# A hybrid attention block: when the steps of three attention branches are written among projections, gates and merges

## The chip, the cores and the metric

The kernel runs on one core of a Trainium2 chip. The core has five engines that work side by side: TensorE (PE in the rows; its weight loads are PEld), VectorE (DVE), ScalarE (ACT), GpSimd (POOL) and SyncE (SP, which here only issues transfers). Each engine takes its instructions in the order in which they stand and waits at each for what it needs. The metric is the device time of one execution in microseconds (us), as the median of several runs.

## What is computed

One layer of a hybrid block on 512 positions of width 1024: a norm, one wide projection, three kinds of attention (A sparse, B with compressed and windowed keys, C dilated), three gates that mix their outputs, an output projection and a gated feed-forward part.

```python
h = _rms(x, norm1_g[layer])
(a_q, a_k, a_v, i_q, i_k, i_w, b_q, b_kv, b_g, c_qkv, mix_g) = _split_last(h @ w_in[layer], IN_SIZES)
...
y_a = _dsa_attention(a_q, a_k, a_v, ..., rel_a) @ w_branch_a[layer]
...
y_b = _nsa_attention(b_q, ..., b_gates, ..., rel_b) @ w_branch_b[layer]
...
y_c = _dilated_attention(_rms(c_qkv[:, :, 0], qk[4]), _rms(c_qkv[:, :, 1], qk[5]), c_qkv[:, :, 2],
                         rel_c) @ w_branch_c[layer]
g = jax.nn.sigmoid(mix_g).reshape(bsz, seq, 3, D_MODEL)
x = x + (g[:, :, 0] * y_a + g[:, :, 1] * y_b + g[:, :, 2] * y_c) @ w_out[layer]
h = _rms(x, norm2_g[layer])
gate, up = jnp.split(h @ w_ffn_in[layer], 2, axis=-1)
x = x + (jax.nn.silu(gate) * up) @ w_ffn_out[layer]
```

The dilated branch has three groups of four heads; a position attends to its near 128 positions, to every 4th of the last 512 and to every 16th of the last 2048, and the three are mixed by their softmax sums.

## The kernel before

**Matmuls.** Each product of two float32 matrices is made of three matmuls (helper `mm3`, lines 106 to 108): both operands are split into a high part (`whi`, `xh`) and a low part (`wlo`, `xl`), and high by high, low by high and high by low are summed in one PSUM tile `pm`. Weights come from DRAM as `raw` (issued by SP, line 93), ACT casts the high part (line 81), and DVE subtracts to get the low part (line 82).

**The projection.** `proj_tm` makes 256 columns of the wide projection for four blocks of 128 positions: for each block a `pm` tile, a copy out of it by ACT, and one call of `tick()`. `spill` uses it for what is written to DRAM and read back later: queries of branch A (`aq_tm`), six pieces of queries and keys of branch C (`cqk_tm`) and three of its values (`cv_tm`).

**Attention as a task.** `attention()` is a generator. `start` puts it in a list of tasks, and each `tick()` moves every task of the list by one step, so what a step emits stands in the program between the matmuls that the caller is emitting. It is started behind the first of the two `aq_tm` projections. Its `pipeline` of units is worked three deep: a step emits part `a` of a new unit, part `b` of the one before it, and `c` of the one before that if there is one. Part `a` makes logits on PE (tile `lg`, lines 363 and 364 for A and B, 838 and 843 for C) and a softmax: DVE adds the bias table and takes the extreme (line 547 by name of the helper `add_table`), ACT takes the exponential, DVE the reciprocal and the normalisation (lines 563, 564 for A and B; 855, 856 for C); in A the bias table is first masked by POOL (`tabm`, line 557). Part `b` transposes the probabilities `p` or `pc_` on PE (tile `tr`, line 111) and copies them out (`pT` by ACT, in C also `pt12` by DVE, line 876). Part `c` makes the products with the values (`ovb`, `ova`, `ovc`). Units of B come first, then A, then C: `c_prep` reads back `c_in` from DRAM (line 755), transposes it on PE, and makes the queries and keys `cqs`, `cks` (split in two by ACT and DVE, lines 765 to 781) and `cq`; it also loads bias tables `ctab` by many small transfers (line 246) and clears three tiles `pt12` on POOL (line 825). Branch C has two halves `hf` of eight units; `c_prep` of the second half is fed in between the units of the first. There are 86 steps in all.

**Gates and merges.** Then come, for the branches in the order B, A, C (`bi` = 1, 0, 2) and eight column blocks `f` each, a `gate` (24 matmuls, `xh` and `xl` against `whi` and `wlo`, with two ticks, then a tanh by ACT into a `tz` tile that shares three buffers of tag `tm`) and a `merge` (12 matmuls of the branch's output `oT`, or 6 for C, then a multiply by DVE; from A on the sum so far is read from `dz` in DRAM and added). The result is stored to `dz` by SP (line 978), but for C, where it stays on chip. Ahead of a branch's first merge `ready(bi)` ticks until the attention outputs of that branch are all there, and ahead of the third until no task is left.

**What sets the order.** The order on each engine comes from the tile framework's scheduler, which runs the program with a model of the engines: of the instructions that are ready it takes by priority, and priority follows the order of emission. Parts `c` stand in `tc.high_priority()`. The logits have two PSUM buffers and the transposes two; `p`, `pc_` and `c_in` share five buffers in SBUF. Output projection and feed-forward come behind all that and have no attention in them.

Of the kernel before, what the change touches and what calls it, by code (L numbers as in the profile page):

```python
# [31 lines left out]
C_CQ, C_CK, C_CV, C_MIX = 2268, 3036, 3804, 4572  # L32
# [35 lines left out]
def block_kernel(ctx: ExitStack, tc: tile.TileContext, x, norm1_g, norm2_g, w_in, qk_norm_g, cmp_pos, cmp_w,  # L68
                 w_ba, w_bb, w_bc, w_out, w_fi, w_fo, rel_bias, onehot, masks, out):
    nc = tc.nc  # L70
# [13 lines left out]
    def weights(w, segs, kcs, per=2, pool=()):  # L84

        res = {}
        width = sum(n for _, n in segs)
        with tc.high_priority():
            for k0 in kcs[::per]:
                raw = wp.tile([128, per, width], F32, name="raw", tag="raw", bufs=5)  # L90
                o = 0
                for c0, n in segs:
                    nc.sync.dma_start(raw[:, :, o:o + n],
                                      w[k0 * 128:(k0 + per) * 128, c0:c0 + n].rearrange("(k p) c -> p k c", p=128))
                    o += n
                hi = wp.tile([128, per, width], F32R, name="whi", tag="whi")
                lo = wp.tile([128, per, width], F32R, name="wlo", tag="wlo")
                split(hi, lo, raw, nc.gpsimd if pool and k0 // per % 4 in pool else None)
                for j in range(per):
                    res[k0 + j] = (hi[:, j, :], lo[:, j, :])  # L100
        return res

    def mm3(ps, pairs, k0=0, n=None):
        n = n or len(pairs)
        for j, ((ah, al), (bh, bl)) in enumerate(pairs, k0):
            nc.tensor.matmul(ps, ah, bh, start=(j == 0), stop=False)  # L106
            nc.tensor.matmul(ps, ah, bl, start=False, stop=False)  # L107
            nc.tensor.matmul(ps, al, bh, start=False, stop=(j == n - 1))  # L108
# [7 lines left out]
    def start(gen):  # L116
        tasks.append(gen)

    def tick():
        for g in list(tasks):  # L120
            try:
                next(g)
            except StopIteration:
                tasks.remove(g)
# [79 lines left out]
    def mm_tile():  # L204
        return mmp.tile([128, S], F32, name="pm", tag="mm")
# [43 lines left out]
        return bass.AP(tensor=tab.tensor, offset=tab.offset + hi - 1, ap=[list(tab.ap[0]), [-1, hi - lo]])  # L249


    def proj_tm(segs, evac, then=None):
        width = sum(n for _, n in segs)
        wk = weights(w_in, segs, list(range(KC)), pool=PP)
        for t in range(NT):
            ps = mm_tile()
            ts = slice(t * 128, (t + 1) * 128)
            mm3(ps[:, 0:width], [((xh[:, k, ts], xl[:, k, ts]), wk[k]) for k in range(KC)])
            evac(t, ps)
            tick()  # L260
        if then is not None:
            start(then())

# [20 lines left out]
    def tmt(name):  # L284
        return ap_.tile([128, NT, 256], F32, name=name, tag="tm", bufs=3)

    def norm_heads(tm, c0, nh):

        ss = ty.tile([128, 16], F32, name="ss", tag="ss")
        v4 = tm[:, :, c0:c0 + 64 * nh].rearrange("p t (h d) -> p t h d", d=64)  # L290
        for t in range(0, NT, 2):
            sq = ap_.tile([128, 2, 256], F32, name="sq", tag="sq", bufs=1)
            nc.scalar.activation(sq[:, :, 0:64 * nh], tm[:, t:t + 2, c0:c0 + 64 * nh], AF.Square)
            nc.vector.tensor_reduce(out=ss[:, t * nh:(t + 2) * nh].rearrange("p (t h) -> p t h", h=nh),
                                    in_=sq[:, :, 0:64 * nh].rearrange("p t (h d) -> p t h d", d=64), op=ALU.add,
                                    axis=AX.X)
        r = rstd(ss, NT * nh, 1.0 / 64)
        r4 = r[:, 0:NT * nh].rearrange("p (t h) -> p t h", h=nh).unsqueeze(3).to_broadcast([128, NT, nh, 64])
        nc.vector.tensor_tensor(out=v4, in0=v4, in1=r4, op=ALU.mult)
# [190 lines left out]
    def b_keys(si):  # L490
        ktm = tmt("bk_tm")
        vv = ab.tile([128, NT, 128], F32, name=f"bv{si}")
        bv[si] = vv

        def evac(t, ps):
            nc.scalar.copy(undup(ktm[:, t, :], 2), dup(ps[:, 0:128], 2))
            nc.vector.tensor_copy(vv[:, t, :], ps[:, 128:256])

        def then():
            norm_heads(ktm, 0, 4)  # L500
            yield from wait(3)
            bk[si] = []
            for g in range(2):
                bk[si].append(k_stack(ktm, 128 * g, gain[:, 3:4]))
                yield

        proj_tm([(C_BKV + 256 * (si + 1), 256)], evac, then=then)
# [224 lines left out]
    dC = dp.tile([6, 128, NT, 256], F32, name="dC")  # L732
    dV = dp.tile([3, S, 256], F32, name="dV")
    cmap = {}

    def spill(name, segs, dst, nh):
        t_ = tmt(name)

        def then():
            if nh:  # L740
                norm_heads(t_, 0, nh)
            nc.sync.dma_start(dst, t_)
            yield

        proj_tm(segs, lambda t, ps: nc.scalar.copy(t_[:, t, :], ps[:, 0:256]), then=then)

    c_in = {}
    c_jobs = [(hf, g, s) for hf in range(2) for g in range(3) for s in "qk"]
# [210 lines left out]
    def merge(bi, f, tz):  # L959
        nk = KC // 2 if bi < 2 else 2  # L960
        os_ = outs[bi]
        cs = slice(128 * (f % 2), 128 * (f % 2) + 128)
        th, zi = tz[:, 0, :], tz[:, 1, :]
        if f % 2 == 0:
            wys["w"] = weights(wbs[bi], [(f // 2 * 256, 256)], list(range(nk)))
        if bi != 1:
            nc.sync.dma_start(zi, dz[f])
        wy = wys["w"]
        py = mm_tile()
        mm3(py, [((wy[k][0][:, cs], wy[k][1][:, cs]), (os_[k][:, 0, :], os_[k][:, 1, :])) for k in range(nk)])  # L970
        if bi == 0 or f % 2:
            tick()
        nc.vector.scalar_tensor_tensor(out=th, in0=th, scalar=1.0, in1=py, op0=ALU.add, op1=ALU.mult)
        if bi != 1:
            eng = nc.vector if bi == 2 and f > KC - 3 else nc.gpsimd
            eng.tensor_tensor(out=th, in0=th, in1=zi, op=ALU.add)
        if bi != 2:
            nc.sync.dma_start(dz[f], th)
        else:
            nc.scalar.mul(zs["h"][:, f, :], th, 0.5)  # L980
            nc.vector.scalar_tensor_tensor(out=zs["l"][:, f, :], in0=th, scalar=0.5, in1=zs["h"][:, f, :].bitcast(F32),
                                           op0=ALU.mult, op1=ALU.subtract)
# [15 lines left out]
    cn = 0  # L998
    for hf in range(2):
        for g in range(3):  # L1000
            spill("cqk_tm", [(C_CQ + 256 * g + 128 * hf, 128), (C_CK + 256 * g + 128 * hf, 128)], dC[cn], 4)
            cmap["q", hf, g], cmap["k", hf, g] = (cn, 0), (cn, 128)
            cn += 1
    for g in range(3):
        spill("cv_tm", [(C_CV + 256 * g, 256)], dV[g].rearrange("(t p) c -> p t c", p=128), 0)
    zx = ExitStack()

    def ready(bi):
# [99 lines left out]
    for c in range(0, DFF, 256):  # L1108
# [7 lines left out]
        for j in range(2):  # L1116
# [7 lines left out]
            f = c // 128 + j  # L1124
# [40 lines left out]
```

## Time and profile before

| | us |
|---|---|
| median of three runs | 996.48 |
| the three runs | 994.18, 996.48, 1000.4 |
| the profiled execution | 995.54 |
| its span on the core | 993.8 |
| PE busy | 974.3 |
| DVE busy | 568.1 |
| ACT busy | 437.5 |
| POOL busy | 175.4 |

The times in the rows are those of the profiled execution, counted from the start of its span. The program's parts lie in it roughly so: norm and first projections to 150, the projections of the dilated branch with attention B from there to 283 and their tail to 308, gates and merges of B with attention A to 446, and gates and merges of A with attention C to 545; the third branch's gates and merges and the rest follow. "Busy" of PE counts an instruction's whole duration, and those of two neighbours overlap; the granted clock is 1.00 at the full 2.4 GHz and 0.50 at 1.2 GHz.

### The profile page before, as it was taken

What the parts mean: (1) busy time and instruction counts of PE and PEld (TensorE: products, weight loads), DVE (VectorE), ACT (ScalarE), POOL (GpSimd) and SP (SyncE); (2) the same over time, 40 slices, a digit from 0 to 9 for tenths busy, and PEclk for the clock granted to TensorE, in tenths of its full rate; (3) what the DMA queues carried; (4) which work ended last, traced back from release to release, by engine and by line L of the source; (5) the groups of instructions that cost most, each with busy time, mean ns of one, the idle gap of its engine ahead of it and who ended that gap; (6) DMA issues with size and microseconds to landing.
All of it is one profiled execution on the core that took longest, in us unless ns stands there. A gap on an engine that the chain in (4) does not pass through costs nothing.

```text
span 993.8 us, 16076 instructions
## 1 busy us (share of the span) xinstructions
PE 974.3 (98%) x5887; PEld 827.0 (83%) x5887; DVE 568.1 (57%) x1277; ACT 437.5 (44%) x956; POOL 175.4 (18%) x156
## 2 busy tenths in 40 slices
PE   6999999999999999989999999999999999999998
PEld 6889999899887578858777899988888888888886
DVE  6699999766665655665764654544344444422321
ACT  5544555755665555554543434433233233322220
POOL 4135555543100202231110312000000000000000
PEclk9999999999999899989999999999999999999999
DMA  8541344433232334346613462233333323332421
GB/s 210 122 128 44 85 119 132 123 109 122 90 104 67 85 117 138 107 141 193 180 62 97 140 210 86 85 94 108 96 85 105 107 85 91 110 97 96 138 75 42
DMA packets 119264, 109.91 MB, mean 111 GB/s; under 512 B 19931, under 2 KB 105234, under 8 KB 119186
## 3 DMA queue, kind: packets, MB, share of 16 engines
q1 hardware_dynamic: 116994, 107.85, 37.4%
q10 hardware_dynamic: 2192, 1.05, 0.4%
q8 instruction: 46, 0.75, 0.3%
q14 instruction: 32, 0.26, 0.1%
HBM read 96.66 MB, written 12.21 MB: 110 GB/s over the span
## 4 chain that ended last, share of the span: by engine, by line
PE 96%; DMA 1%; DVE 1%; ACT 1%; issue 0%; SPq 0%; DVEq 0%; ACTq 0%
PE pf L108 14%; PE pf L107 14%; PE pf L106 14%; PE pm L107 13%; PE pm L106 13%; PE pm L108 13%; PE tr L111 5%; PE ovb L541 2%; PE lg L363 2%; PE lg L364 2%; PE ova L541 1%; PE lg L843 1%; DMA raw<-in_w_in 1%; PE ovc L888 1%; PE lg L838 0%
## 5 line engine op out<-in xcount | busy, mean ns | idle before, releaser
L82 DVE TENSOR_TENSOR wlo<-raw,whi 128x512 fp32r<-128x512 f32 (+1 forms) x243 | 182.5, 756 | 147.7 <-ACT whi L81 146.6
L81 ACT CAST whi<-raw 128x512 fp32r<-128x512 f32 (+1 forms) x288 | 176.8, 619 | 173.9 <-PE pf L108 78.6
L107 PE MATMUL pm<-wlo,xh 128*128 128x256 f32 (+1 forms) x512 | 145.9, 288 | 0.3 <-DVE wlo L82 0.3
L108 PE MATMUL pm<-whi,xl 128*128 128x256 f32 (+1 forms) x512 | 145.3, 286 | 0.5 <-POOL xl L82 0.5
L106 PE MATMUL pm<-whi,xh 128*128 128x256 f32 (+1 forms) x512 | 145.7, 289 | 0.0
L107 PE MATMUL pf<-xl,whi 128*128 128x512 f32 (+1 forms) x384 | 142.6, 372 | 0.1
L106 PE MATMUL pf<-xh,whi 128*128 128x512 f32 (+1 forms) x384 | 142.5, 372 | 0.0
L108 PE MATMUL pf<-xh,wlo 128*128 128x512 f32 (+1 forms) x384 | 142.0, 371 | 0.0
L107 PEld LDWEIGHTS pm<-wlo,xh 128*128 128x128 f32 x512 | 98.5, 193 | 1.9 <-issue 0.8
L108 PEld LDWEIGHTS pm<-whi,xl 128*128 128x128 f32 x512 | 98.7, 193 | 1.4 <-POOL xl L82 0.8
L106 PEld LDWEIGHTS pm<-whi,xh 128*128 128x128 f32 x512 | 98.3, 194 | 0.4
L107 PE MATMUL pm<-xl,whi 128*128 128x512 f32 x224 | 88.8, 396 | 0.0
L108 PE MATMUL pm<-xh,wlo 128*128 128x512 f32 x224 | 88.6, 395 | 0.0
L106 PE MATMUL pm<-xh,whi 128*128 128x512 f32 x224 | 88.4, 395 | 0.0
L107 PEld LDWEIGHTS pf<-xl,whi 128*128 128x128 f32 x384 | 72.3, 188 | 12.8 <-DVE xl L82 0.3
L108 PEld LDWEIGHTS pf<-xh,wlo 128*128 128x128 f32 x384 | 72.2, 188 | 12.6
L106 PEld LDWEIGHTS pf<-xh,whi 128*128 128x128 f32 x384 | 72.2, 188 | 12.3
L82 POOL TENSOR_TENSOR wlo<-raw,whi 128x512 fp32r<-128x512 f32 x45 | 62.2, 1402 | 111.6 <-ACT whi L81 100.8
L106 PE MATMUL pf<-whi,hh 128*128 128x512 f32 x176 | 69.4, 395 | 0.0
L108 PE MATMUL pf<-whi,hl 128*128 128x512 f32 x176 | 69.4, 395 | 0.0
L107 PE MATMUL pf<-wlo,hh 128*128 128x512 f32 x176 | 69.4, 395 | 0.0
L562 ACT ACTIVATE p<-p,m 128x128 f32<-128x128 f32 (+3 forms) x96 | 53.9, 562 | 28.6 <-DVE m L547 26.4
(312 smaller groups left out, 1702.3 us busy)
## 6 DMA issues: line engine op xcount, KB each, us to landing
raw<-in_w_in SPq DMA_DIRECT2D x92, 256.0 KB, 3.0
raw<-in_w_ffn_in SPq DMA_DIRECT2D x88, 256.0 KB, 2.9
raw<-in_w_ffn_out SPq DMA_DIRECT2D x44, 256.0 KB, 2.8
raw<-in_w_in SPq DMA_DIRECT2D x52, 128.0 KB, 2.4
x<-in_x SPq DMA_DIRECT2D x8, 512.0 KB, 5.9
tab<-dvec SPq DMA_DIRECT2D x16, 256.0 KB, 3.3
dz<-tz SPq DMA_DIRECT2D x16, 256.0 KB, 2.4
tz<-dz SPq DMA_DIRECT2D x16, 256.0 KB, 3.3
```

The costliest lines, as they stand in the source:

```text
L81: nc.scalar.copy(dst_hi, src)
L82: (eng or nc.vector).tensor_tensor(out=dst_lo, in0=src, in1=dst_hi.bitcast(F32), op=ALU.subtract)
L106: nc.tensor.matmul(ps, ah, bh, start=(j == 0), stop=False)
L107: nc.tensor.matmul(ps, ah, bl, start=False, stop=False)
L108: nc.tensor.matmul(ps, al, bh, start=False, stop=(j == n - 1))
L111: nc.tensor.transpose(dst, src, ident[0:src.shape[0], 0:src.shape[0]])
L363: nc.tensor.matmul(lg, qs, k[:, 0, 0:w], start=True, stop=False)
L364: nc.tensor.matmul(lg, qs, k[:, 1, 0:w], start=False, stop=stop)
L541: mm = nc.tensor.matmul(ov[64 * j:64 * j + 64, 128 * b:S], v(b), pts[j][:, 4 * b:3 * b + NT, :], start=first and b == 0, stop=last and b = ...
L562: nc.scalar.activation(p[:, 0:w], p[:, 0:w], AF.Exp, bias=m[:, 0:1], scale=-1.0, accum_out=m[:, 1:2])
L843: nc.tensor.matmul(lg[32 * r:32 * r + 32, c:c + n], ld["q", g][hp, 128 * i + 32 * r:128 * i + 32 * r + 32], ld["k", g][hp, 128 * r:128 * r ...
L888: nc.tensor.matmul(ov[h, 128 * b_:128 * q1], ld["v", 0][:, b_, h], d["pt", jj][:, 2 * b_:b_ + q1, :], start=b_ == 0, stop=False)
```

## The change

`proj_tm` gets an argument `more`: in the first `more` of its four blocks two ticks are called instead of one. `spill` hands it on, and the nine spills of the dilated branch pass 1, so each of these projections emits five steps of the tasks where it emitted four. In `merge` the tick is called always; before, the merges of `bi` = 1 and `bi` = 2 called it only for odd `f`. In the merges of `bi` = 2 there is no task left to step. Nothing else is different; no instruction is added or removed.

```diff
--- before.py
+++ after.py
@@ -249,7 +249,7 @@
         return bass.AP(tensor=tab.tensor, offset=tab.offset + hi - 1, ap=[list(tab.ap[0]), [-1, hi - lo]])
 
 
-    def proj_tm(segs, evac, then=None):
+    def proj_tm(segs, evac, then=None, more=0):
         width = sum(n for _, n in segs)
         wk = weights(w_in, segs, list(range(KC)), pool=PP)
         for t in range(NT):
@@ -257,7 +257,8 @@
             ts = slice(t * 128, (t + 1) * 128)
             mm3(ps[:, 0:width], [((xh[:, k, ts], xl[:, k, ts]), wk[k]) for k in range(KC)])
             evac(t, ps)
-            tick()
+            for _ in range(1 + (t < more)):
+                tick()
         if then is not None:
             start(then())
 
@@ -733,7 +734,7 @@
     dV = dp.tile([3, S, 256], F32, name="dV")
     cmap = {}
 
-    def spill(name, segs, dst, nh):
+    def spill(name, segs, dst, nh, more=0):
         t_ = tmt(name)
 
         def then():
@@ -742,7 +743,7 @@
             nc.sync.dma_start(dst, t_)
             yield
 
-        proj_tm(segs, lambda t, ps: nc.scalar.copy(t_[:, t, :], ps[:, 0:256]), then=then)
+        proj_tm(segs, lambda t, ps: nc.scalar.copy(t_[:, t, :], ps[:, 0:256]), then=then, more=more)
 
     c_in = {}
     c_jobs = [(hf, g, s) for hf in range(2) for g in range(3) for s in "qk"]
@@ -968,8 +969,7 @@
         wy = wys["w"]
         py = mm_tile()
         mm3(py, [((wy[k][0][:, cs], wy[k][1][:, cs]), (os_[k][:, 0, :], os_[k][:, 1, :])) for k in range(nk)])
-        if bi == 0 or f % 2:
-            tick()
+        tick()
         nc.vector.scalar_tensor_tensor(out=th, in0=th, scalar=1.0, in1=py, op0=ALU.add, op1=ALU.mult)
         if bi != 1:
             eng = nc.vector if bi == 2 and f > KC - 3 else nc.gpsimd
@@ -998,11 +998,11 @@
     cn = 0
     for hf in range(2):
         for g in range(3):
-            spill("cqk_tm", [(C_CQ + 256 * g + 128 * hf, 128), (C_CK + 256 * g + 128 * hf, 128)], dC[cn], 4)
+            spill("cqk_tm", [(C_CQ + 256 * g + 128 * hf, 128), (C_CK + 256 * g + 128 * hf, 128)], dC[cn], 4, 1)
             cmap["q", hf, g], cmap["k", hf, g] = (cn, 0), (cn, 128)
             cn += 1
     for g in range(3):
-        spill("cv_tm", [(C_CV + 256 * g, 256)], dV[g].rearrange("(t p) c -> p t c", p=128), 0)
+        spill("cv_tm", [(C_CV + 256 * g, 256)], dV[g].rearrange("(t p) c -> p t c", p=128), 0, 1)
     zx = ExitStack()
 
     def ready(bi):
```

By the code, 49 steps of attention have been emitted at the end of the projections where 40 had, 53 ahead of the first merge where 44 had, and 77 ahead of the first merge of the second branch where 64 had. Attention has no step left from the merge f = 3 of the second branch on; before, that was f = 7.

The next rows show where that moved instructions and where not. Numbers behind names count tiles in the order of the program and so differ between the two; lines behind the first part of the file are one higher after the change. The first place is PE where the last units of branch A stand ahead of the gates: logits of A, transposes of its probabilities, one transpose of a `c_in`, the product. Before:

```order
L363 MATMUL lg_5260<-kst_823,qst_5000 128x512
L364 MATMUL lg_5260<-kst_823,qst_5000 128x512
L111 MATMUL tr_5239<-ident_82,p_5207 128x128 x3
L111 MATMUL tr_5244<-ident_82,p_5218 128x128 x3
L111 MATMUL tr_5287<-ident_82,p_5254 128x128 x4
L111 MATMUL tr_5293<-ident_82,p_5265 128x128 x4
L111 MATMUL tr_5408<-ident_82,c_in_5283 128x128 x4
L541 MATMUL ova_5377<-pT_5137,av_248 64x512
```

After:

```order
L364 MATMUL lg_5020<-kst_823,qst_4787 128x512
L365 MATMUL lg_5020<-kst_823,qst_4787 128x512
L111 MATMUL tr_4999<-ident_82,p_4967 128x128 x3
L111 MATMUL tr_5004<-ident_82,p_4978 128x128 x3
L111 MATMUL tr_5047<-ident_82,p_5014 128x128 x4
L111 MATMUL tr_5053<-ident_82,p_5025 128x128 x4
L111 MATMUL tr_5153<-ident_82,c_in_5043 128x128 x4
L542 MATMUL ova_5125<-pT_4897,av_248 64x512
```

The rows are the same but for numbers, and so are all of PE's 687 instructions around them, from the first logits behind the third product of branch B on to row 2564 below.

The second place is PE behind it, at the head of the units of branch C. `pm_6026` before and `pm_6314` after are the same gate, `cq`, `cqs` and `cks` the prepared queries and keys. Before:

```order
L111 MATMUL tr_5555<-ident_82,c_in_5474 128x128 x4
L107 MATMUL pm_5953<-oT_5386,whi_5776 128x512
L108 MATMUL pm_5953<-oT_5386,wlo_5777 128x512
L106 MATMUL pm_6026<-xh_105,whi_5833 128x512
L107 MATMUL pm_6026<-xl_106,whi_5833 128x512
L108 MATMUL pm_6026<-xh_105,wlo_5834 128x512
L111 MATMUL tr_5574<-ident_82,c_in_5511 128x128 x4
L843 MATMUL lg_5642<-cq_5509,cq_5472 32x32 x4
L843 MATMUL lg_5700<-cq_5509,cq_5472 32x32 x4
L106 MATMUL pm_6026<-xh_105,whi_5833 128x512
L107 MATMUL pm_6026<-xl_106,whi_5833 128x512
L108 MATMUL pm_6026<-xh_105,wlo_5834 128x512
```

After, where the rows on from 2568 to 2603 (36 of them) are all of this kind, transposes, logits and one product, and the gate's first matmul is row 2604:

```order
L111 MATMUL tr_5274<-ident_82,c_in_5222 128x128 x4
L107 MATMUL pm_6298<-oT_5134,whi_6190 128x512
L108 MATMUL pm_6298<-oT_5134,wlo_6191 128x512
L111 MATMUL tr_5320<-ident_82,c_in_5243 128x128 x4
L844 MATMUL lg_5384<-cq_5241,cq_5220 32x32 x4
L844 MATMUL lg_5441<-cq_5241,cq_5220 32x32 x4
L111 MATMUL tr_5373<-ident_82,c_in_5371 128x128 x4
L844 MATMUL lg_5384<-cq_5325,cq_5279 32x32 x4
L844 MATMUL lg_5441<-cq_5325,cq_5279 32x32 x4
L839 MATMUL lg_5492<-cks_5186,cqs_5158 128x256 x2
L844 MATMUL lg_5492<-cq_5241,cq_5220 32x64 x4
L844 MATMUL lg_5492<-cq_5325,cq_5279 32x64 x4
```

Before, the gate's matmuls stand among the transposes and logits; after, they stand behind 36 rows of attention. From the gate on, attention and gates alternate as before, in fewer and longer pieces (18 changes from attention to a gate or merge where there were 27), up to about 545 us by the rows of before.

The third place is SP, which issues the transfers. `dz<-tz` are stores of merged sums, `c_in` and `ctab` loads for branch C's second half, `raw` weights, `c_v` its values. Before:

```order
L755 DMA c_in_5629<-dC_254 128x4x128
L978 DMA dz_256<-tz_5476 128x512
L93 DMA raw_6203<-in_w_in 128x2x256
L813 DMA c_v_5730<-dV_255 128x4x128
L978 DMA dz_256<-tz_5581 128x512
L813 DMA c_v_5868<-dV_255 128x4x128
L967 DMA tz_5766<-dz_256 128x512
L93 DMA raw_6405<-in_w_branch_a 128x2x256
L813 DMA c_v_5966<-dV_255 128x4x128
```

After:

```order
L756 DMA c_in_5585<-dC_254 128x4x128
L246 DMA ctab_5721<-dvec_247 32x128
L246 DMA ctab_5721<-dvec_247 32x256
L246 DMA ctab_5721<-dvec_247 32x128 x2
L756 DMA c_in_5658<-dC_254 128x4x128
L246 DMA ctab_5721<-dvec_247 32x256
L246 DMA ctab_5721<-dvec_247 32x128 x2
L978 DMA dz_256<-tz_5761 128x512
L978 DMA dz_256<-tz_5906 128x512
L978 DMA dz_256<-tz_6061 128x512
L968 DMA tz_6180<-dz_256 128x512
```

The stores to `dz` stood between the loads and now stand three in a row behind the last `ctab` and `c_in` loads of the second half.

## Rows read from the trace of the kernel before

**Rows 1.** The page's first part: busy us, share of the span, instructions, by engine

```profile
PE 974.3 (98%) x5887; PEld 827.0 (83%) x5887; DVE 568.1 (57%) x1277; ACT 437.5 (44%) x956; POOL 175.4 (18%) x156
```

**Rows 2.** Table by stage: window, length, busy us by engine, PEclk, DMA share, GB/s

```profile
150.00:308.00 158.00, 158.00 (x1195) 143.98 (x1193) 109.18 (x308) 95.16 (x256) 49.94 (x36) 1.00 0.37 108
...
324.00:340.00 16.00, 13.82 (x73) 7.93 (x70) 7.81 (x27) 8.42 (x23) 0.67 (x1) 0.79 0.18 55
...
430.00:446.00 16.00, 11.45 (x54) 6.89 (x53) 10.39 (x19) 7.44 (x17) 4.50 (x6) 0.79 0.53 150
...
459.00:545.00 86.00, 85.94 (x681) 64.70 (x680) 52.90 (x153) 39.86 (x89) 7.84 (x6) 1.00 0.46 139
```

**Rows 3.** The same table in slices of 2 us, in both holes

```profile
328.00:330.00 2.00, 1.04 (x7) 0.73 (x7) 1.07 (x6) 2.00 (x8) 0.00 (x0) 1.00 0.63 181
...
336.00:338.00 2.00, 2.00 (x12) 1.12 (x10) 0.00 (x0) 0.00 (x0) 0.00 (x0) 0.50 0.00 0
...
436.00:438.00 2.00, 1.27 (x6) 0.80 (x6) 1.60 (x7) 1.89 (x5) 0.00 (x0) 0.50 0.06 18
```

**Rows 4.** Timeline, all engines, 430 to 437: start, length, engine, line, operation, [idle before]

```profile
431.37 4.02 DVE L564 TENSOR_SCALAR p<-p,m 128x384 f32<-128x384 f32 x1
...
432.44 2.74 POOL L825 MEMSET pt<- 128x1024 f32 x3
...
435.54 0.87 PE L111 MATMUL tr<-ident,p 128*128 128x128 f32 x3 [3.49 <-DVE p L564]
...
436.59 0.41 DVE L564 TENSOR_SCALAR p<-p,m 128x384 f32<-128x384 f32 x1
```

**Rows 5.** Operations on tile `cv_tm`: ns min/median/max, first and last start

```profile
L745 ACT COPY cv_tm<-pm x12: 347/365/376, 227.3 to 282.6; 128x256 f32<-128x256 f32 x12
```

**Rows 6.** Chain of waits, 301 to 312: start, length, what

```profile
308.34 2.31 PE ovb L541 x16
```

**Rows 7.** Timeline, 168 to 170

```profile
168.28 0.33 DVE L633 TENSOR_TENSOR pc<-pc,mc 128x128 f32<-128x128 f32 x1
...
169.22 0.27 PE L111 MATMUL tr<-ident,pc 128*128 128x128 f32 x1
```

**Rows 8.** Chain of waits, 455 to 545, units of branch C

```profile
472.25 0.43 PE lg L838 x2
472.68 0.36 PE lg L843 x16
473.04 0.43 PE pm L108
473.47 0.23 PE pm L106
...
484.57 0.44 PE tr L111 x4
```

**Rows 9.** Groups by line and shape, 440 to 545: busy us, mean ns, idle before

```profile
L781 DVE SCALAR_TENSOR_TENSOR cks<-tr,gain_qk,cks 64x512 fp32r<-64x512 f32 x8 | 6.0, 748 | 0.1
...
L956 ACT ACTIVATE tz<-pm 128x512 f32<-128x512 f32 x8 | 4.8, 596 | 13.2 <-PE pm L108 6.8 <-DMA dz<-tz 5.6 <-POOL tz L976 0.7
...
L766 DVE TENSOR_TENSOR cqs<-tr,cqs 64x512 fp32r<-64x512 f32 x4 | 2.8, 689 | 0.1
...
L855 DVE RECIPROCAL mcc<-mcc 128x1 f32<-128x1 f32 x16 | 2.6, 160 | 1.9 <-ACT pc__6057 L854 0.9 <-ACT pc__6318 L854 0.6 <-ACT pc__6175 L854 0.2
...
L876 DVE COPY pt<-tr 64x128 f32<-64x128 f32 x8 | 2.3, 286 | 0.1
```

**Rows 10.** Timeline of DVE, 491 to 493

```profile
492.09 0.48 DVE L547 CUSTOM_DVE_ANT_1 pc__6016<-lg,ctab,mcc 128x256 f32<-128x256 f32 x1
492.50 0.08 DVE L547 DVE_READ_ACCUMULATOR2_ANT mcc<- 128x1 f32 x1
```

**Rows 11.** Timeline of SP, 456 to 459

```profile
457.54 0.53 SPq L755 DMA_DIRECT2D c_in<-dC  x1
```

**Rows 12.** DMA issues: count, KB each, median us to landing

```profile
c_in<-dC SPq DMA_DIRECT2D x12, 256.0 KB, 3.4
```

## The prediction, made before the kernel was run

> **What bounds the kernel now.** I read the page's list of engines first. PE is busy 98% of the span and nothing else is over 57% [rows 1], so the change can only give or cost what PE idles, what it works at the lower clock, and what its pieces lose where they alternate. The table by stage says where that is [rows 2]: PE is busy all of 150 to 308 us. It has lost time at 324 to 340 (13.82 of 16 busy, granted clock 0.79) and at 430 to 446 (11.45 of 16, clock 0.79); then it is full again from 459 to 545 (85.94 of 86), the stretch in which attention's third branch lies between gates and merges.
>
> The two holes come from the short tails of branches B and A, where PE has only attention left and each step waits for the one ahead of it. Slices of 2 us show PE falling to 1.04 busy and the clock at 0.50 behind it, up to 338 [rows 3]. In the second hole the timeline gives the cause: a DVE normalisation that takes 0.41 us next to it took 4.02 us, while POOL ran a masked table and three clears of `pt12` one behind the other, up to 435.2; PE stood 3.49 us for it [rows 4]. The price of a hole is the idle time and half of the work done at half clock. A mean clock of 0.79 over 16 us is 0.21 x 16 / 0.5 = 6.7 us at 0.50, in each. The first: 16 - 13.82 = 2.2 us idle, and PE full in the slow part (2.00 of 2 at 336 [rows 3]), some 6.4 us of work, so 3.2; together 5.4. The second: 16 - 11.45 = 4.55 idle, and the slow part only some 60% full (1.27 of 2 at 436 [rows 3]), 4 us of work, so 2.0; together 6.6. All a better placing of attention can win here is about 12 us.
>
> **Is emission the limit?** The last copy of the last projection of the dilated branch lies at 282.6 us [rows 5], and by the code 40 attention steps have been emitted by then, the third product of branch B (step 36) among them; that product runs at 308.34 us [rows 6], some 25 us later. Attention runs behind its emission already, held by its own chain (logits, DVE, exp, DVE, transpose, copy) and its buffers, not by when it was written. More steps emitted ahead then change priorities in the scheduler and not the pace, and the order shows just that.
>
> **The change, part by part.** (1) Nine more steps in the nine projections, one each, and four more in the merges of the first branch (f = 0, 2, 4, 6); the eight merges of the third have no task left. No instruction is added or removed on any engine; no price of its own.
>
> (2) 150 to 308 us. The order moves by a few rows only: each logits group up to some 40 matmuls earlier, each transpose about as far behind. PE had no idle here [rows 2]. The tightest hand-over I find is DVE's compressed probabilities, done at 168.28 + 0.33, read by PE at 169.22: 0.6 us of slack [rows 7]. In the new order DVE has up to 1.1 us more ahead of the same transpose, so PE may wait 0 to 0.5 us there. I take 0.3.
>
> (3) 308 to 459 us. On PE the rows from the first logits behind the third product to the merge ahead of the dilated queries' transposes are the same 687 instructions in the same order, on DVE, ACT, POOL and SP likewise (the order pieces show the end of the second hole), and their waits lead to the same producers. The clears of `pt12` stand where they stood. Both holes stay: gain 0. What would have been the win of this change (12 us) is not in it.
>
> (4) 459 us on. Here the order does change (the second pair of pieces). Before, the units of the dilated branch lay between gate matmuls; now 36 rows of attention stand in one run, from the transpose of `c_in_5243` to the next gate, with no gate or merge matmul among them. PE's own work in the run is 38 transposes at 0.11 (0.44 for four) and the logits of eight units, whole or in part (0.43 for the wide pair, 0.18 and more for eight narrow ones), with one product: 4.2 and some 6 us, with the changes between them 10.5 [rows 8]. What it waits for is DVE, in order. With two logits buffers PE may not write the third group before DVE has read the first. From the first read up to that of the seventh unit, DVE has 12 reads of logits (0.48 for the widest, 5.3 by their widths), 12 accumulators (0.08: 1.0), 6 reciprocals (1.0), 6 normalisations (about 0.41 [rows 4]: 2.4), 6 copies to `pt12` (1.7), 2 splits of `cqs` (1.4) and 4 of `cks` (3.0), durations from [rows 9, 10]: 15.8 us. DVE starts each some 0.05 before the one ahead has ended (0.48 from 492.09, the next at 492.50 [rows 10]), so 14. It waits three times for ACT (an exp, twice `cks`), by the tanh's 0.60 [rows 9] 1.9 in all. Behind that stand one more exp and the gate's tanh, 0.6 to 0.7 each, which frees the PSUM tile that the next gate needs, and some 0.5 of hand-overs: 17.3 to 18 us from the first read to the gate. PE has its 10.5 in that time and idles 7. Ahead of it the transpose of `c_in_5371` waits: SP issued the load in its place at 457.54 before [rows 11], behind 24 `ctab` loads; one store ahead of it is gone, so 457.0; it lands 3.4 us later, at 460.4 [rows 12], and PE is there at 459.5: 0.9. Together 7.9 us. Below: DVE's 14 alone, 3.3. Above: no overlap on DVE, 9.7.
>
> (5) The stores `dz<-tz` have moved on SP behind all of the second half's `ctab` and `c_in` loads (third pair). The tanh named above needs a `tm` buffer, free when a store has landed: at 0.53 an issue [rows 11] SP gets there at about 475, and a store has landed by 478.4 if it needs what a load needs [rows 12]; the tanh is due at 477.8. About even; I take nothing, up to 1 more.
>
> (6) The clock. In both holes PE stood, in short pieces in the first and for 3.49 us in the second [rows 4], and its clock was at 0.50 for some 6.7 us afterwards. In the run the 7.9 us fall, queue by queue, into some nine waits of 0.3 to 1.7 us within 19 us, PE 58% busy. In the first hole PE was about half busy ahead of the fall [rows 3]. If it falls here for 6.7 us, 58% of that is 3.9 us of work at half speed, 3.9 us at most where all is on the path, 0 where DVE hides it. I take the middle, 2. The Trainium skill (TensorE: Matmul & The Clock Gate, What's actually happening) has the array throttled only after an idle window and released by activity; read to the letter, waits broken by work would keep the clock up and the sum would be 2 less. The first hole speaks against that reading: the 2 us ahead of its fall hold seven instructions and 1.04 us of work [rows 3]. So the rows decide.
>
> (7) PE goes from attention to gate and merge matmuls 27 times in this stretch before and 18 times after. A first matmul behind logits holds the chain for 0.43, others for 0.23; behind transposes none is longer [rows 8]. So each of the 9 gives between 0 and 0.20; I take 0.08, a gain of 0.7. Behind that the rest of attention is spread between gates again, as now, and the gates and merges that follow stand alone; PE is full in the stretch that has both [rows 2], so nothing more is lost or won.
>
> Sum on the profiled execution's 995.54 us (span 993.8): + 0.3 + 7.9 + 2 - 0.7 = 1005.0. That execution is 0.9 us under the median of the runs, 996.48; a measurement of this kernel tells about 1% from no change, 986.5 to 1006.4.
>
> **Rivals.** *The holes close.* If attention really came earlier, both holes would fill: 995.5 - 12 = 984, faster. For it: that is where the only idle time is. Against: the order there is the same row by row. What could still do it is the clears' timing: the Trainium skill (SBUF — State Buffer, Who interferes with whom) gives DVE and GpSimd one port pair that either locks for a whole instruction, and the 4.02 us row agrees. Should the normalisation start ahead of POOL's row, 3.6 us of wait and some 2 of slow clock go: 995.5 + 9.5 - 5.6 = 999.4. The point that decides is which of the two starts first at 431.3; nothing ahead of it moves. Chance for a result under 986.5: 0.06.
>
> *The run costs little.* DVE's 14 us alone and no fall of the clock, or the holes' own luck as above: 995.5 + 3.3 - 0.7 = 998 to 1001. For it: hand-overs overlap more than I count. Chance 0.27.
>
> *The run costs more.* All bounds up, and the clock falls twice, or the stores of (5) come 2 us late and gates wait for `tm` buffers: 995.5 + 0.5 + 9.7 + 1 + 3.9 = 1010.6. For it: the second hole cost more than its chain of durations. Against: POOL is idle in the run, so no DVE row is stretched. Chance 0.15.
>
> **The numbers.** Forecast 0.52, 1005, own range 1002 to 1008, of which a little under half (0.22) lies above 1006.4. Faster 0.06; slower 0.22 + 0.15 = 0.37; within 1% 0.30 + 0.27 = 0.57. The range 998 to 1011 leaves out 0.06 below, and some 0.1 at the two ends.
>
> **What would show it.** In the profile after: the wait of 3.5 us for the normalisation and both stretches of clock 0.50 as before (3); PE under 60% busy for some 19 us from about 459, its waits on DVE and ACT at transposes and logits of the dilated branch, DVE nearly full in it (4); a third stretch at 0.50 near 465 to 475 (6); PE full elsewhere. It would be wrong if the holes are gone, if DVE is idle while PE waits in the run (then SP's loads were late), or if PE idles between 150 and 308.

## The result and the profile after

Five executions of the changed kernel took 1005.26 to 1007.41 us, median 1007.12; five of the kernel before had a median of 994.68. The ratio is 1.0109, with a 95% interval of 1.0090 to 1.0129: slower by about 1%. The forecast was 1005.0 with 998 to 1011, and the place and the sign were right. Several parts of the sum were not, as the stages show.

The profiled execution took 1006.88 us. The page's first lines, which answer to [rows 1]: the span is 11.3 us longer with the same number of matmuls.

```profile
span 1005.1 us, 16082 instructions
...
PE 977.7 (97%) x5887; PEld 830.3 (83%) x5887; DVE 561.3 (56%) x1277; ACT 438.4 (44%) x956; POOL 175.5 (17%) x156
```

The table by stage, which answers to [rows 2] (columns as there):

```profile
150.00:308.00 158.00, 156.86 (x1187) 142.69 (x1186) 104.43 (x301) 93.32 (x250) 51.21 (x36) 1.00 0.36 107
...
324.00:340.00 16.00, 13.57 (x85) 8.30 (x84) 10.35 (x37) 10.87 (x33) 2.05 (x3) 1.00 0.24 67
...
430.00:446.00 16.00, 11.49 (x51) 6.78 (x50) 9.51 (x16) 7.66 (x17) 4.30 (x5) 0.79 0.57 161
446.00:459.00 13.00, 12.75 (x81) 10.41 (x79) 6.03 (x9) 4.71 (x8) 3.07 (x3) 1.00 0.33 80
459.00:545.00 86.00, 80.27 (x611) 60.59 (x612) 49.20 (x149) 37.84 (x84) 7.74 (x6) 0.86 0.42 123
```

PE has lost 1.14 us in 150 to 308, where it lost none. The first hole is as empty as before (13.57 of 16 busy) but its granted clock stayed at 1.00. The second hole is the one of before (11.49, 0.79). In 459 to 545 PE, full before, is 80.27 of 86 busy at a mean clock of 0.86.

Fixed points of the order say how much each stage took. The third product of branch B in the chain of waits, which answers to [rows 6], starts at 309.61 where it started at 308.34, 1.3 us late:

```profile
309.61 2.31 PE ovb L542 x16
```

The last product of branch A on PE's timeline, the changed kernel's row and then that of before, is 1.6 us early, so the first hole gave back 2.9:

```profile
438.99 3.22 PE L542 MATMUL ova<-pT,av 128*64 128x512 f32 x16
```

```profile
440.59 2.37 PE L541 MATMUL ova<-pT,av 128*64 128x512 f32 x16
```

Its 3.22 us against 2.37 are the low clock of the second hole, which costs 0.85 more here. So the kernel comes out of it 0.8 us early and ends 11.3 us late: **12.1 us are lost among the units of branch C**.

PE's timeline of the long stretch, 457 to 484 (start, length, operation, in brackets the idle time before it and what ended it), shows its waits: 0.65 + 1.58 + 2.10 + 0.56 + 0.78 + 0.31 = 6.0 us.

```profile
457.93 0.60 PE L111 MATMUL tr<-ident,c_in 128*128 128x128 f32 x4
...
459.40 0.63 PE L111 MATMUL tr<-ident,c_in 128*128 128x128 f32 x4 [0.65 <-DMA c_in<-dC]
...
461.83 0.77 PE L839 MATMUL lg<-cks,cqs 128*128 128x256 f32 x2 [1.58 <-DVE mcc L548]
...
466.59 1.11 PE L111 MATMUL tr<-ident,c_in 128*128 128x128 f32 x4 [2.10 <-DMA c_in<-dC]
...
471.43 1.09 PE L111 MATMUL tr<-ident,c_in 128*128 128x128 f32 x4 [0.56 <-issue]
473.30 0.69 PE L111 MATMUL tr<-ident,pc__5452 128*128 128x128 f32 x2 [0.78 <-DMA ctab<-dvec]
...
475.23 0.88 PE L111 MATMUL tr<-ident,pc__5503 128*128 128x128 f32 x3 [0.31 <-DVE pt L877]
...
483.56 0.79 PE L106 MATMUL pm<-xh,whi 128*128 128x512 f32 x1
```

Three of them, 3.5 us, the profile puts down to a transfer (`c_in`, `c_in`, `ctab`). DVE's timeline says the same of the longest from the other side: it had finished at 465.7 and stood for 2.48 us, until 468.17.

```profile
465.26 0.42 DVE L857 TENSOR_SCALAR pc__5503<-pc__5503,mcc 128x384 f32<-128x384 f32 x1
468.17 0.42 DVE L548 CUSTOM_DVE_ANT_0 pc__5549<-lg,ctab 128x256 f32<-128x256 f32 x1 [2.48 <-PE tr L111]
```

The load behind it in the chain of waits: SP went from issue to issue without a pause and came to this `c_in` at 461.36, and the data took 5.19 us. That is 1.0 over the median of 4.2 for this kernel's twelve such loads, with the DMA engines all but full (shares of 0.82 to 1.04 from 460 to 466, two of these slices below), so part of the lateness is the transfer's own.

```profile
460.35 0.42 SPq L246
...
461.36 5.19 DMA c_in<-dC
```

Slices of 2 us show the clock: at 0.50 from some 461.2 to 485, and for the last 9 us of it with PE full.

```profile
458.00:460.00 2.00, 1.35 (x32) 0.93 (x33) 0.69 (x1) 1.44 (x3) 0.00 (x0) 1.00 1.06 303
460.00:462.00 2.00, 0.42 (x18) 0.34 (x18) 1.56 (x8) 1.16 (x3) 0.00 (x0) 0.80 0.82 217
...
464.00:466.00 2.00, 0.49 (x16) 0.24 (x12) 1.06 (x5) 0.71 (x2) 0.00 (x0) 0.50 0.95 266
...
476.00:478.00 2.00, 2.00 (x22) 1.36 (x22) 1.82 (x9) 1.42 (x5) 0.00 (x0) 0.50 0.59 161
...
482.00:484.00 2.00, 2.00 (x16) 1.82 (x16) 1.76 (x7) 1.28 (x3) 0.00 (x0) 0.50 0.92 283
484.00:486.00 2.00, 2.00 (x8) 1.53 (x8) 1.48 (x5) 1.25 (x4) 1.28 (x1) 0.73 0.22 83
```

By the mean of the 86 us, (1 - 0.86) x 86 / 0.5 = 24 us at half clock. PE's own work from the transposes at 457.93 to the gate at 483.56, forecast at 10.5 us, took 25.6 - 6.0 = 19.6. So the slow clock cost about 9 us, say 8 to 10, and the waits 6.0; that is 2 to 4 more than the 12.1 lost, which the fewer changes between attention and gates, and the gates that now stand alone, gave back. That part has not been measured by itself.

### The profile page after: what moved, and what is told of

Same layout as the page of the kernel before. It is cut to its first block, busy times and chain, and to the rows that moved or that the text cites. A ratio compares the mean times of both kernels' runs of the same rounds, so it can differ in the third digit from the quotient of the medians.

```text
span 1005.1 us, 16082 instructions
## 1 busy us (share of the span) xinstructions
PE 977.7 (97%) x5887; PEld 830.3 (83%) x5887; DVE 561.3 (56%) x1277; ACT 438.4 (44%) x956; POOL 175.5 (17%) x156
## 4 chain that ended last, share of the span: by engine, by line
PE 91%; DVE 3%; DMA 3%; issue 1%; SPq 1%; ACT 1%; POOL 1%; DVEq 0%; POOLq 0%; ACTq 0%
PE pf L108 14%; PE pf L107 13%; PE pf L106 13%; PE pm L107 12%; PE pm L106 12%; PE pm L108 12%; PE tr L111 5%; PE ovb L542 2%; PE lg L364 2%; PE lg L365 2%; PE ova L542 1%; DMA raw<-in_w_in 1%; PE lg L844 1%; PE ovc L889 1%; DMA c_in<-dC 1%
## 5 line engine op out<-in xcount | busy, mean ns | idle before, releaser
L82 DVE TENSOR_TENSOR wlo<-raw,whi 128x512 fp32r<-128x512 f32 (+1 forms) x243 | 176.1, 730 | 151.4 <-ACT whi L81 150.1
```

The source lines that it names most:

```text
L82: (eng or nc.vector).tensor_tensor(out=dst_lo, in0=src, in1=dst_hi.bitcast(F32), op=ALU.subtract)
```

## The experiments

The theory going in: one long stretch of attention without gates makes PE wait for DVE, and the waits bring the clock down. The rivals: SP's late loads; the number of steps as such; the clock as something apart. All kernels compare with the kernel before on the same chip; its median there was 996.03 for the first four, 994.42 for the next four, and 994.19 for the last two.

**Each part alone.** The kernel before with only the second part of the change:

```diff
-        if bi == 0 or f % 2:
-            tick()
+        tick()
```

> The kernel before with one part of the change alone: a tick in every merge, no extra tick in the projections. PE's order is that of before up to the units of branch C, and among these no stretch of attention longer than 46 matmuls and transposes stands between two gates (121 in the changed kernel). Theory of the prediction (the loss sits in that one long stretch): nothing is lost, 993 to 997 us as before, and PE waits under 1 us from 459 to 545. Rival (each extra step costs its share of the 11 us, 4 of 13 steps): about 998.5 us, with new waits of some 3 us at transposes of branch C.

Measured: 994.71 us, ratio 0.9989 (0.9969 to 1.0009): no change. The theory's forecast held. The other part alone was not run: built without the ticks in the merges, the changed kernel has every engine's instructions in the same order, row for row. So the projections' steps are the whole change. With fewer of them, counted from the first projection, the order is the changed kernel's from five extra steps on; with three or four it is one and the same again, and the first stretch in branch C has 44 matmuls and transposes instead of 121. Four, in the first four projections:

```diff
-            spill("cqk_tm", [...], dC[cn], 4, 1)
+            spill("cqk_tm", [...], dC[cn], 4, int(cn < 4))
...
-        spill("cv_tm", [...], ..., 0, 1)
+        spill("cv_tm", [...], ..., 0, 0)
```

> The changed kernel with the extra step in only the first four of the nine projections (merges all tick). PE's order up to the units of branch C is then that of the changed kernel, but the first stretch of attention there has 44 matmuls and transposes between gates, not 121; with five or more extra steps the order is the changed kernel's to the row. Theory (the loss is that one stretch, through waits and the clock): 994 to 998 us, granted clock of the span above 0.990, and only the 1.5 us of waits at the compressed branch's transposes are left of the loss. Rival (the loss grows with the steps, four of nine): about 1001.

Measured: 1001.68, ratio 1.0061 (1.0040 to 1.0082). The theory in this form fell: 44 rows cost too, and the rival's figure was met. The waits of PE (total, times, longest) hold the 1.6 us for the first reads of the logits, as in the long stretch, and a gate that waits for the tanh, which in turn waits for a store to `dz`:

```profile
PE pm L106 <- ACT tz L957: 2.9, 2, 2.2
PE lg L839 <- DVE mcc L548: 1.6, 1, 1.6
```

To part the stretch from what lies ahead of it, three steps in the value projections, where the order up to branch C is that of before:

```diff
-            spill("cqk_tm", [...], dC[cn], 4, 1)
+            spill("cqk_tm", [...], dC[cn], 4, 0)
```

> The changed kernel with the extra step in the three value projections only (merges all tick). PE's order up to the units of branch C is that of before, row for row; the first stretch of attention in branch C has 44 rows of one matmul between gates, as with four steps (1001.7 us). Theory (that stretch costs by itself, and of the loss with four steps only the 1.2 us at the compressed branch's transposes belongs elsewhere): 999 to 1001.5 us, with the wait of 1.6 us for the first reads of the logits, a gate's wait for the tanh, and one fall of the clock in 459 to 485. Rival (with four steps it was the earlier reordering that cost most, and 44 rows cost nothing): 994 to 997, as with the merges alone.

Measured: 998.88, ratio 1.0045 (1.0031 to 1.0060), just under what the theory gave. Its stretch has the same 1.6 us wait and a mean clock of 0.82 over 28 us, 10 us at 0.50:

```profile
457.00:485.00 28.00, 24.24 (x197) 18.38 (x197) 18.13 (x55) 14.63 (x32) 1.18 (x1) 0.82 0.73 209
```

So the ratio goes 0.9989, 1.0045, 1.0061, 1.0109 with 0, 3, 4 and 9 steps. The times alone fit the rival that each step costs its share; the order does not, since the steps beyond the fifth change no row and it jumps between four and five. The kernels with three and four steps differ in where the steps stand, and their intervals overlap, so that four cost more than three is not shown.

**What PE waits for.** The changed kernel with the second half's loads on POOL's queue:

```diff
-            nc.sync.dma_start(t_, dC[n, :, :, c0:c0 + 128])
+            (nc.gpsimd if hf else nc.sync).dma_start(t_, dC[n, :, :, c0:c0 + 128])
```

> The changed kernel with the six loads c_in of branch C's second half issued by POOL instead of SP, so that they no longer stand behind the 24 small ctab transfers; the long stretch of attention stays (108 rows of one matmul each where there were 121). Theory of the prediction (DVE, in order, sets the pace): it gains at most 1 us, 1006 to 1008, the waits move to DVE's results. Rival (SP's late loads set it: waits of 0.65, 2.10, 0.56 and 0.78 us ended by a DMA in the changed kernel): 4 us of waits go and with a shorter half-clock stretch 2 to 5 us more, 998 to 1002. If POOL issues each transfer much more slowly than SP, the waits at c_in grow instead, over 1009.

Measured: 1004.49 (ratio 1.0095, 1.0069 to 1.0120), between the two forecasts. The waits of 457 to 486 that are left all end with an engine; the `c_in` waits are gone, and the 0.78 us at 473.30, which the profile had put down to a `ctab` load, stayed and is now put down to ACT's `cq`:

```profile
PE lg L839 <- DVE mcc L548: 1.8, 1, 1.8
PE tr L111 <- ACT cq L807: 0.8, 1, 0.8
PE tr L111 <- issue: 0.6, 1, 0.6
PE tr L111 <- DVE pt L877: 0.3, 1, 0.3
PE lg L844 <- ACT cq L807: 0.2, 1, 0.2
```

So SP's queue was 2.8 us of the waits, which fell from 6.0 to 3.7 in all. By the medians 2.6 us came off, but the two kernels were not measured side by side and the intervals of their ratios overlap, so the size of the gain is not secured. The clock did not come back sooner by much: it is at 0.50 from 461 to 482 in this kernel, with PE full from 462 on but for 1.7 us. Two slices show it there, PE full and the clock low:

```profile
476.00:478.00 2.00, 2.00 (x7) 0.83 (x5) 1.75 (x7) 1.53 (x4) 0.00 (x0) 0.50 0.92 263
478.00:480.00 2.00, 2.00 (x19) 1.31 (x19) 1.04 (x4) 0.81 (x2) 1.27 (x1) 0.50 0.74 254
```

Next, also DVE's copies to ACT:

```diff
-                    nc.vector.tensor_copy(ld["pt", j][0:n, g, i, :], ps[r0:r0 + n, 2, :])
+                    nc.scalar.copy(ld["pt", j][0:n, g, i, :], ps[r0:r0 + n, 2, :])
```

(and the other of the two copies alike.)

> The changed kernel with c_in of the second half issued by POOL (as in e3_cin_pool, 1004.5) and with branch C's copies into pt12 on ACT instead of DVE: 1.7 us less in DVE's chain over the long stretch. Theory of the prediction (DVE's chain paces what is left of the waits): 1.5 us or more off, 1001 to 1003. Rival (the low clock is most of the loss and a little less waiting does not end it): 1003.5 to 1005.5. If ACT becomes late in DVE's place, over 1005.5, with new waits ended by ACT.

Measured: 1002.01 (1.0070, 1.0044 to 1.0096), the figure of the theory of DVE's chain: 2.5 us less by the medians for 1.7 us off DVE, though the intervals overlap here too. The way there is not the one that the theory took. PE's waits in the stretch went only from 3.7 to 3.1 us; what got shorter is the slow part, from some 20.5 to 13.4 us ((1 - 0.76) x 28 / 0.5):

```profile
457.00:485.00 28.00, 24.87 (x235) 18.21 (x234) 18.96 (x60) 19.97 (x48) 4.76 (x5) 0.76 0.63 189
```

So each theory holds in part: SP's queue held PE for 2.8 us, DVE's copies for some 0.6, and the rest of the difference goes with the clock.

**The clock.** Can work in PE's waits keep the clock up? First, the near logits twice, in the place where they are computed:

```diff
-            for c in range(2):
+            for c in (0, 1, 0, 1) if hf == 0 else (0, 1):
```

> The changed kernel with the near logits of branch C's first half computed twice, one over the other (16 more matmuls of 256 columns, 0.43 us a pair, 3.4 us in all): only work is added. Theory A (PE waits there anyway, and its low clock comes from its waits): the added work lies in waits, PE's share in 459 to 485 rises from some 70 to 80%, the 24 us at clock 0.50 become 7 or fewer, and the time falls to 1000 to 1004. Theory B (the clock is not moved by so little): the work is hidden in waits only in part and runs at half clock, 1008 to 1013.

Measured: 1010.39 (1.0144, 1.0113 to 1.0175), theory B. The added matmuls stand behind the waits and not in them: PE still waits 1.6 and 2.1 us. The test was of the wrong place. So, matmuls that can run while a transpose waits:

```diff
+    def filled(ps, n):
+        for _ in range(n):
+            nc.tensor.matmul(ps.rearrange("p a b -> p (a b)"), xh[:, 0, 0:128], xh[:, 0, :], start=True, stop=True)
+        return ps
...
-            ps = tr_tile()
+            ps = filled(tr_tile(), 0 if hf else 2)
```

(in `tr_cols` alike, for `c_in` of the second half.)

> The changed kernel with two matmuls of 512 columns, whose result is overwritten, put ahead of each transpose of the second half's c_in and of the first half's probabilities in branch C, into the same PSUM tile: 28 matmuls of 0.23 us, 6.4 us of added work, which can run while the transpose waits. Theory A (the low clock is PE's answer to its waits): PE is busier than 85% in 459 to 485, the stretch at 0.50 falls from 24 us to under 12, and the time is 1000 to 1006 in spite of the work. Theory B (what sets the low clock is not how long PE waits there, or the fill does not reach the wait of 1.6 us at which it begins): the low stretch is as long or longer, and the time 1009 to 1014.

Measured: 1007.84 (1.0128, 1.0112 to 1.0144), 0.7 us more than the changed kernel with 6.4 us more work in it: between the theories. PE's timeline has the start of the stretch at 457.12, the first added matmuls, the long wait for `c_in`, and the gate behind the stretch at 482.91; in the changed kernel the stretch lasts from 457.93 to 483.56:

```profile
457.12 0.60 PE L111 MATMUL tr<-ident,c_in 128*128 128x128 f32 x4
...
457.87 0.73 PE L304 MATMUL tr<-xh 128*128 128x512 f32 x2
...
465.47 1.11 PE L111 MATMUL tr<-ident,c_in 128*128 128x128 f32 x4 [2.87 <-DMA c_in<-dC]
...
482.91 0.50 PE L106 MATMUL pm<-xh,whi 128*128 128x512 f32 x1
```

The table of 457 to 483, of this kernel and then of the changed one: PE as busy, the clock 0.80 against 0.58.

```profile
457.00:483.00 26.00, 20.85 (x213) 14.89 (x211) 15.71 (x58) 14.34 (x33) 0.00 (x0) 0.80 0.60 174
```

```profile
457.00:483.00 26.00, 20.02 (x189) 14.10 (x187) 15.76 (x58) 14.07 (x31) 0.00 (x0) 0.58 0.63 178
```

Twenty of the 28 matmuls, 4.6 us of work, lie in the stretch, and it is as long with them (25.8 us against 25.6): the slow part fell from 22 to 10 us ((1 - 0.80) x 26 / 0.5). So theory A's forecast of the clock held, but not its time and not its reason. The time was too good, because the other eight stand where PE was full, and the clock still was low behind the 2.87 us at `c_in`. The reason was that PE would wait less and be over 85% busy in 459 to 485; it was 80% busy, against 78% in the changed kernel, and waited 5.1 us against 6.0. What the added matmuls changed most is the kind of work: matmuls of 512 columns among transposes and narrow logits. No run parts that from the waits. Two runs above keep the question open: with the loads on POOL the clock stayed at 0.50 until 482 though PE had no wait behind 473.1, and with the copies on ACT as well it came back at 475 under attention alone. So the clock fell in a wait; what kept it down for so long is not shown.

**The second hole.** Is it the clears on POOL? The kernel before with them on DVE:

```diff
-            nc.gpsimd.memset(pt, 0.0)
+            nc.vector.memset(pt, 0.0)
```

> The kernel before with the four clears of pt12 on DVE instead of POOL. Theory (the second hole is the normalisation held by POOL's table and clears): it takes 0.41 us instead of 4.02, the wait of 3.49 us goes and with it the fall of the clock, against 3 clears on DVE of some 0.6 to 1.1 us each, of which part lies on the chain: 989 to 993 us. Rival (the normalisation was slow for the masked table alone, or for another reason): it still takes over 2 us, and with the clears in DVE's queue the time is 995 to 998.

Measured: 999.54 (1.0035, 1.0016 to 1.0054), slower, which neither theory had. But the wait went much as the first said: the normalisation that took 4.02 us [rows 4] takes 1.35 and not the 0.41 that was expected, with POOL's table of 1.16 us still beside it. The 2.67 us that went are about the 2.74 of the three clears. PE's wait for it falls from 3.49 to 0.82, and DVE's clears stand behind it at 0.91 each.

```profile
428.11 1.35 DVE L564 TENSOR_SCALAR p<-p,m 128x384 f32<-128x384 f32 x1
...
432.86 0.91 DVE L825 MEMSET pt<- 128x1024 f32 x1 [0.16 <-issue]
```

The gain was lost behind it: PE then waited for `cks` of DVE and for `c_in`.

```profile
PE tr L111 <- DMA c_in<-dC: 2.4, 1, 2.4
PE lg L838 <- DVE cks L781: 1.2, 1, 1.2
...
PE tr L111 <- DVE p L564: 0.8, 1, 0.8
```

On ACT, which is free in the hole:

```diff
-            nc.gpsimd.memset(pt, 0.0)
+            nc.scalar.activation(pt.rearrange("p a b c -> p (a b) c"),
+                                 ident[:, None, :].to_broadcast([128, 2 * NT, 128]), AF.Copy, scale=0.0)
```

> The kernel before with the four clears of pt12 on ACT, which waits in the second hole, instead of POOL. With the clears on DVE the wait of 3.49 us fell to 0.82, but 999.5 us came out, with later waits at c_in (2.4) and cks (1.2). Theory (the wait goes here too, but attention then meets its own loads early, since SP issues them no sooner): wait at the normalisation under 1 us, 995 to 1000 us. Rival (it was DVE's 0.91 us a clear that cost it): 990 to 994.

Measured: 991.62 (0.9972, 0.9950 to 0.9995), faster than before by a narrow margin. The rival was right: the clears cost where they took DVE's own time. With the second half's `c_in` on POOL as well:

> The kernel before with the clears of pt12 on ACT (991.6 us, 0.9972 of before) and also the second half's c_in loads issued by POOL, which stands idle: two waits at c_in of 1.2 us together are left with the clears on ACT. Theory (the loads are late for SP's queue alone): both go, 989.5 to 991.5. Rival (a load issued by POOL is late in its own way, or the transposes then wait for DVE): 991.5 to 993.

Measured: 990.79 (0.9957, 0.9939 to 0.9975), as the theory said, with 0.2 us left at `c_in` and branch C without a gap:

```profile
428.00:446.00 18.00, 15.16 (x71) 9.93 (x70) 9.90 (x23) 12.17 (x23) 4.66 (x4) 0.91 0.64 188
...
457.00:485.00 28.00, 28.00 (x230) 21.73 (x229) 21.11 (x55) 14.99 (x32) 8.03 (x8) 1.00 0.69 204
```

That is the fastest version seen: the kernel before, 3.4 us faster by the medians on the same chip, and by the two ratios 1.5% under the changed kernel.

## Why the prediction was right, and where its working was not

**Emission is not the limit: right.** The order says it, and so do the experiments: both holes are there after the change, the wait for the normalisation included (3.50 us at 433.87), and five extra steps make the same program as nine. The rival in which the holes close had no part in it.

**Step 2, the projections: too small.** 0.3 us was taken, 0.5 the most; it was 1.1 in two waits (0.34 and 0.80). The slack of 0.6 us [rows 7] was counted against DVE's rows in front; missed was how long they take. One that takes 0.15 us before took 1.24, beside a weight split on POOL:

```profile
166.78 1.54 POOL L82 TENSOR_TENSOR wlo<-raw,whi 128x512 fp32r<-128x512 f32 x1 [1.60 <-ACT whi L81]
...
167.11 1.24 DVE L633 TENSOR_TENSOR mc<-mc,bgt 128x4 f32<-128x4 f32 x1
...
168.82 0.30 PE L111 MATMUL tr<-ident,pc 128*128 128x128 f32 x1 [0.80 <-DVE pc L634]
```

The same operation before, on the same view:

```profile
168.09 0.15 DVE L632 TENSOR_TENSOR mc<-mc,bgt 128x4 f32<-128x4 f32 x1
```

**Step 3, the holes stay: right,** but the first cost 2.9 us less, since the clock did not fall there. Its waits are the same (0.72, 0.42, 0.68 and one for the product), 1.26 us later in time. It is not an effect of the order, as one execution of each shows: with four steps the hole has the changed kernel's order and place in time to 0.1 us, and the clock fell; with three it has the order of before, 0.2 us earlier, and the clock stayed up. PE's row of the product in the hole, in the changed kernel and with four steps:

```profile
333.99 2.37 PE L542 MATMUL ovb<-pT,bv 128*64 128x512 f32 x16 [0.52 <-ACT pT L531]
```

```profile
334.39 4.54 PE L542 MATMUL ovb<-pT,bv 128*64 128x512 f32 x16 [0.36 <-ACT pT L531]
```

**Step 4, the waits: 7.9 forecast, 6.0 measured.** The place and the first wait, for the third group of logits, are as written; from the first read at 460.29 to the gate at 483.56 it took 23.3 us where 17.3 to 18 was forecast; the rest is slow clock and late loads, and no run parts the two. The working put 7.0 on DVE and ACT and 0.9 on one load. By the runs 2.8 belonged to loads late in SP's queue: 0.65 to the one load of the working, and 2.10 to a second `c_in`, whose place behind the `ctab` issues was not followed. "DVE idle while PE waits" was named as what would show the working wrong, and it was so for 2.5 us.

**Step 5, the stores: right;** no wait for a `tm` buffer shows in the long stretch (with four steps one does: the tanh, 2.2 us).

**Step 6, the clock: the mis-sized term.** 2 us was taken, for one slow stretch of 6.7 us as in the holes. It was 24 us long and cost 8 to 10. The working let the clock come back 6.7 us after it fell; in the changed kernel new waits followed up to 475.2, and it came back only at 485, after 9 us more in which PE was full.

**Step 7:** 0.7 us of gain from fewer changes, at most 1.8; what the stretch gave back in all is 2 to 4, by difference only.

So a total within 2.1 us came of errors in both directions: waits 2 too high, the clock 6 or more too low, the first hole 2.9 and the savings too low as gains. That they nearly cancel is luck, the first hole's clock above all. The forecast also gave a result within 1% the larger chance (0.57, against 0.37 for slower), and the measured 1.0109 (1.0090 to 1.0129) lies on that line. The time lies in the likeliest case's own range, 1002 to 1008, in the part above 1006.4 that counted as slower.

## What to carry to other kernels

Where an in-order engine is 98% busy, a change of priorities has little to win (here some 12 us in two holes) and can lose as much: look in the new order for a stretch in which it has a single kind of dependent work, and follow every queue that feeds the stretch, the issuing engine's too, not only the longest chain of arithmetic. Do not price the clock by one earlier fall: in the holes it came back after some 6.7 us, in the long stretch after 24, and the last 9 of these had no wait in them. A step off the path that holds up another engine (here clears on POOL, beside which a DVE row took 4.02 us instead of 1.35) can be worth more than the reorderings tried here: moving it took 2.8 us off the median.

## What the runs showed of the hardware

The granted clock differs from one execution to the next of the same program. In 38 executions of the kernel before its mean lay between 0.989 and 0.998, and the span between 989.9 and 998.0 us: a line through them is 989.1 us and 0.91 us more for each us of missing clock ((1 - mean clock) x span). So most of the spread of this kernel's times goes with the clock; that the missing clock lies in the holes is seen in the one profiled execution. The changed kernel's five lay at 0.984 to 0.986, as they would if its long stretch falls each time. The Trainium skill (TensorE: Matmul & The Clock Gate, What's actually happening) says that how many matmuls run slow at a kernel's start varies from run to run of one kernel. The first hole, in the middle of a kernel, with the same waits and either clock, agrees.

A tiny DVE operation, 128 x 4, took 1.24 us instead of 0.15 beside POOL's 1.54 us split of weights, and a normalisation of a shape that takes 0.41 with POOL at rest [rows 4] took 4.02 beside four POOL rows, a table of 1.16 and three clears of 2.74 together, and 1.35 beside the table alone once the clears were on DVE. The Trainium skill (SBUF — State Buffer, Who interferes with whom) has whichever of the two engines comes first hold a shared pair of ports for a whole instruction, for the kinds of instruction that use it. That DVE waits through several POOL instructions in a row is more than it says; here it stood for a table and three clears.
